# The fourth mixer in another order: index scores first, then the latent, then eight heads' queries between the rounds of the choice

## The chip, the core and the metric

The kernel runs on one core of a Trainium2 chip. TensorE (PE in the profile, its weight loads PEld) multiplies matrices into PSUM banks; VectorE (DVE), ScalarE (ACT) and GpSimd (POOL) do the element-wise work; SyncE (SP) issues the transfers from HBM. Each engine has its own queue of instructions and works it off strictly in order; an instruction waits until what it reads is written and the buffer that it writes is free. The metric is the device time of one execution in microseconds (us). The kernel before took 1725.35 us (median of 3 runs, 1724.01 to 1725.73).

## The reference

Two networks are computed one after the other, two layers each, on 256 tokens of width 1024 (272 tokens in the second network, which puts 16 learned tokens in front). Each layer has a mixer and a gated feed-forward block. The change is in the mixer of the last layer, the fourth mixer of the program. What it computes, cut to what matters:

```python
c_q, c_kv, k_idx, w_idx = split(h @ w_in, [256, 512, 576])
c_q, c_kv = rms_norm(c_q, g0), rms_norm(c_kv, g1)
q_abs, q_idx = split(c_q @ w_uq, [16 * 256])          # 16 heads of 256; 8 index heads of 64
q_abs = rms_norm(q_abs.reshape(b, t, 16, 256), q_norm)
k_idx = rms_norm(k_idx)
act = relu(einsum("bqhd,bsd->bqhs", q_idx, k_idx) * 64 ** -0.5)
score = where(visible, einsum("bqh,bqhs->bqs", w_idx * 8 ** -0.5, act), -1e30)
_, sel = top_k(score, 64)                              # 64 keys for each query
kv = gather(c_kv, sel)
logits = einsum("bqhr,bqkr->bqhk", q_abs, kv) / 16 + bias
p = softmax(where(visible, logits, -1e30))
o = einsum("bqhr,hrd->bqhd", einsum("bqhk,bqkr->bqhr", p, kv), w_uv)
h = h + o @ w_out
```

So a query of the attention (`q_abs`) needs only `c_q`. The scores need `c_q`, `k_idx` and `w_idx`. The latent `c_kv` is needed for the logits and the values, and the choice of 64 keys only for the softmax.

## The kernel before

All activations lie feature by token. Weights come in chunks of up to 1 MB in the order of `stream_plan`; three chunk buffers (`raw`) hold them, five pairs of buffers hold the pieces of up to 1024 columns after they are split into a high part `wh` (ACT, L189) and a low part `wl` (L191, on DVE, or on POOL for the pieces that `ON_POOL` lists). A product of two float32 matrices is three matmuls (`mm3`, L214 to L216). `take` hands out the next piece, `ahead` splits up to four pieces beyond it.

`dsa_mix` is the fourth mixer. It has eight PSUM banks: `mm` 2, `s` 2, `b` 1, `n` 1, `o` 2. In its text it does in turn:

- `c_q`: matmuls with `bw`, scaling (`latent`), sum of squares, norm, split into `cqh` and `cql`.
- The index key `ki` with `bwi`, and its norm over 64 features (matmul with `blk` into an `n` bank).
- The latent `c_kv` with `bw2` (two matrices of 24 matmuls each): scaled into `lat` by DVE, squares, norm, a product on POOL, then `ckg` (keys with all gains) and `ckv` (split, for the values).
- The index weights `wi` with `bwx`, transposed into `wc`.
- The index queries `qi` with `uqi`, and the scores: for each of 8 index heads two matmuls (L222) into an `s` and an `o` bank, relu on ACT (`rl`, L1086), and a weighted sum on DVE (`sc`, L1091 and L1093).
- The choice: eight rounds (`top_rounds`), each with MAX8 and MATCH_REPLACE8 on both halves of the queries (L1106, L1107). Where a score was taken out, `msk` is 1e30 afterwards (L1216, L1217).
- `prep(h)`, one head's query: 12 matmuls into an `mm` bank, squares on ACT with their sums in `qst` (L1150), the inverse root by `rsq`, scaling out of the bank into `qx` (ACT for a head with `h < 2`, L1154, else DVE, L1156), four transposes on PE (L1160, bank `n`), and a copy into `q` on ACT (L1162). The bank stays taken from the first matmul to the scaling, so two heads can be under way.
- `rsq` has two ways. With `pool` set, ACT computes a logarithm, a second small term (L253) and an exponential, POOL does three tiny products (L257 to L259) and DVE the last step (L260). Without it DVE does three steps (L263 to L265).
- `values(g)`: the values of four heads, three products of 6 matmuls and copies on ACT (L1123, L1126).
- `mask(h)`: the bias tile `nb` of a head comes by DMA (three buffers), and POOL adds `msk` (L1167).
- `attend(h)`: logits into an `s` bank (L1179), bias and row minimum on DVE (L1181), exponential on ACT (L1183), reciprocal on DVE (L1185), product on POOL (L1187), transposes into bank `b` (L979 to L982), copy `pr` on ACT (L984), and for each second head the product with the values (`o`, L222).

Before the change the text has the first four heads' queries one by one between pairs of rounds, then `values(0)`, and the loop over the heads prepares head h + 4 (`LAG`) beside head h. The order in the text isn't the order on the engines: the program is built with a scheduler that puts the instructions in an order for each engine by its own estimate of times, and that order is then fixed.

## Time and profile before

| | |
|---|---|
| time, median of 3 | 1725.35 us |
| the profiled execution | 1724.67 us |
| its span, first to last instruction | 1722.9 us |
| mean granted clock of TensorE | 0.991 |
| fourth mixer, first to last matmul | 1379.7 us to 1523.3 us of the span |
| in it: longest time without a matmul | 5.63 us, from 1411.45 us |

The profiled execution lies 0.68 us under the median; 1.77 us of it lie outside the span. TensorE is busy nearly everywhere. The mixer is some 140 us of the span, and what a change in it is worth is read there: at which places TensorE has no matmul to do, and what it waited for. A clock of 0.5 in a row means that TensorE was granted the lower of its two levels (1.2 GHz), 1.0 the higher (2.4 GHz).

### The profile page before, as it was taken

How to read it: one execution, taken by the hardware profiler on the slowest of the kernel's cores; microseconds unless marked ns; L12 is line 12 of the kernel's file. 1: busy time of each engine (PE TensorE's matmuls, PEld its weight loads, DVE VectorE, ACT ScalarE, POOL GpSimd, SP SyncE). 2: the span in 40 equal slices, each digit the busy share in tenths (PEclk: the TensorE clock that was granted, in tenths of full speed). 3: DMA queues.
4: the chain of work that ended last, by engine and by line, in shares of the span. 5: the costliest groups of instructions: out<-in, count | busy, mean ns of one | idle time of the engine just before them, and what ended most of it. 6: DMA issues, size and time to landing. Idle time of an engine off the chain costs nothing.

```text
span 1722.9 us, 32907 instructions
## 1 busy us (share of the span) xinstructions
PE 1682.0 (98%) x13474; PEld 1638.4 (95%) x13474; DVE 1095.4 (64%) x1789; ACT 898.6 (52%) x1559; POOL 417.9 (24%) x426
## 2 busy tenths in 40 slices
PE   8999999999999999999999999999999989999999
PEld 7999999988999999999997899999999978889999
DVE  7757666565666566655787666556665586566653
ACT  6545455476544554444576554444444457755442
POOL 3023220013322022211333522211221135342210
PEclk9999999999999999999999999999999999999999
DMA  7456655434455545444542354454555433345552
GB/s 278 145 189 229 228 194 177 169 105 141 160 183 194 176 171 192 174 171 172 187 145 67 135 184 172 172 176 172 178 177 180 143 112 108 111 151 192 185 189 92
DMA packets 59926, 287.54 MB, mean 167 GB/s; under 512 B 12112, under 2 KB 22864, under 8 KB 29184
## 3 DMA queue, kind: packets, MB, share of 16 engines
q1 hardware_dynamic: 58944, 284.80, 47.7%
q8 instruction: 105, 1.72, 0.4%
q10 hardware_dynamic: 832, 0.66, 0.1%
q14 instruction: 45, 0.37, 0.1%
HBM read 284.34 MB, written 5.53 MB: 168 GB/s over the span
## 4 chain that ended last, share of the span: by engine, by line
PE 93%; DVE 3%; ACT 1%; issue 1%; DMA 1%; SPq 0%; POOL 0%; ACTq 0%; DVEq 0%; POOLq 0%
PE mm L214 21%; PE mm L215 21%; PE mm L216 21%; PE z L216 7%; PE z L215 7%; PE z L214 7%; DVE xl L231 1%; PE s L1179 1%; PE o L222 1%; PE z L222 1%; DMA X<-in_xT_dram 1%; PE s L222 1%; PE o L918 0%; PE n L849 0%; DVE X L390 0%
## 5 line engine op out<-in xcount | busy, mean ns | idle before, releaser
L189 ACT CAST wh<-raw 128x1024 fp32r<-128x1024 f32 (+1 forms) x526 | 541.9, 1032 | 622.9 <-PE mm L215 409.7
L191 DVE TENSOR_TENSOR wl<-raw,wh 128x1024 fp32r<-128x1024 f32 (+2 forms) x494 | 600.3, 1217 | 322.0 <-ACT wh L189 318.2
L214 PE MATMUL mm<-xh,wh 128*128 128x256 f32 (+1 forms) x1808 | 523.9, 290 | 15.1 <-ACT xh L226 4.7
L215 PE MATMUL mm<-xl,wh 128*128 128x256 f32 (+1 forms) x1808 | 520.2, 288 | 0.7 <-DVE xl L231 0.4
L216 PE MATMUL mm<-xh,wl 128*128 128x256 f32 (+1 forms) x1808 | 519.9, 288 | 0.0
L214 PEld LDWEIGHTS mm<-xh,wh 128*128 128x128 f32 x1808 | 342.8, 190 | 21.8 <-ACT xh L226 5.3
L215 PEld LDWEIGHTS mm<-xl,wh 128*128 128x128 f32 x1808 | 342.6, 190 | 5.1 <-issue 2.3
L216 PEld LDWEIGHTS mm<-xh,wl 128*128 128x128 f32 x1808 | 343.5, 190 | 1.0 <-issue 0.5
L215 PE MATMUL z<-xl,wh 128*128 128x256 f32 (+1 forms) x1056 | 302.0, 286 | 1.4 <-DVE xl L231 1.3
L216 PE MATMUL z<-xh,wl 128*128 128x256 f32 (+1 forms) x1056 | 302.0, 286 | 0.0
L214 PE MATMUL z<-xh,wh 128*128 128x256 f32 (+1 forms) x1056 | 301.2, 285 | 0.0
L214 PE MATMUL mm<-gh,wh 128*128 128x256 f32 (+1 forms) x1056 | 300.5, 285 | 0.0
L216 PE MATMUL mm<-gh,wl 128*128 128x256 f32 (+1 forms) x1056 | 299.5, 284 | 0.0
L215 PE MATMUL mm<-gl,wh 128*128 128x256 f32 (+1 forms) x1056 | 299.5, 284 | 0.0
L346 POOL TENSOR_TENSOR es<-es,r 128x256 f32<-128x256 f32 (+1 forms) x110 | 152.4, 1387 | 476.2 <-ACT es L345 476.2
L215 PEld LDWEIGHTS z<-xl,wh 128*128 128x128 f32 x1056 | 199.1, 189 | 2.0 <-DVE xl L231 1.9
L216 PEld LDWEIGHTS z<-xh,wl 128*128 128x128 f32 x1056 | 199.7, 189 | 0.2
L214 PEld LDWEIGHTS z<-xh,wh 128*128 128x128 f32 x1056 | 199.6, 189 | 0.1
L215 PEld LDWEIGHTS mm<-gl,wh 128*128 128x128 f32 x1056 | 199.2, 189 | 0.0
L216 PEld LDWEIGHTS mm<-gh,wl 128*128 128x128 f32 x1056 | 198.5, 188 | 0.0
L214 PEld LDWEIGHTS mm<-gh,wh 128*128 128x128 f32 x1056 | 198.3, 188 | 0.0
L347 DVE TENSOR_TENSOR ea<-z,es 128x256 f32<-128x256 f32 (+1 forms) x132 | 57.1, 433 | 97.7 <-POOL es L346 49.0
(361 smaller groups left out, 1846.1 us busy)
## 6 DMA issues: line engine op xcount, KB each, us to landing
raw<-in_gu_dram SPq DMA_DIRECT2D x132, 1024.0 KB, 4.8
raw<-in_wd_dram SPq DMA_DIRECT2D x66, 1024.0 KB, 4.8
raw<-in_aw_dram SPq DMA_DIRECT2D x12, 1024.0 KB, 4.8
raw<-in_a_in_dram SPq DMA_DIRECT2D x9, 1024.0 KB, 5.3
raw<-in_wo_dram SPq DMA_DIRECT2D x12, 768.0 KB, 4.2
nb<-scr SPq DMA_DIRECT2D x32, 136.0 KB, 2.2
scr<-relrow SPq DMA_DIRECT2D x16, 271.5 KB, 5.3
raw<-in_mkv_dram SPq DMA_DIRECT2D x4, 1024.0 KB, 5.0
```

What stands on the lines that cost most here:

```text
L189: self.nc.scalar.copy(h[:, :c], t[:, x : x + c])
L191: eng.tensor_tensor(l[:, :c], t[:, x : x + c], h[:, :c].bitcast(F32), ALU.subtract)
L214: mm(out, wh, xh, start=first, stop=False, skip_group_check=chk)
L215: mm(out, wh, xl, start=False, stop=False, skip_group_check=chk)
L216: mm(out, wl, xh, start=False, stop=last, skip_group_check=chk)
L222: self.nc.tensor.matmul(out, w, x, start=start, stop=stop, skip_group_check=True)
L231: self.nc.vector.scalar_tensor_tensor(l, src, col, h.bitcast(F32), ALU.mult, ALU.subtract)
L346: nc.gpsimd.tensor_tensor(s, s, r, ALU.mult)
L347: nc.vector.tensor_tensor(a, B[:, :cols], s, ALU.mult)
L1179: nc.tensor.matmul(s[:, c], q[:, k, qc], ckg[:, k, k0 : k0 + n], start=k == 0, stop=k == 1)
```

## The change

- The latent with `bw2` moves in the text from behind the index key to behind the scores, ahead of the queries. Its weights move in the stream from the third place to behind `uqi`.
- All of the first eight heads' queries stand between the rounds of the choice: two ahead of them, two behind each pair of rounds (`LAG` 8 in place of 4). `values(0)` comes behind the last round.
- These eight heads take the `pool` way of `rsq` and are scaled by ACT (before: two heads). In that way the last step moves from DVE to POOL, with one more small instruction on ACT.
- POOL splits the weights of the first eight heads' queries (four pieces, before two) and the first piece of the value weights.

```diff
-ON_POOL = {("uq", 0, 0), ("uq", 1, 0), ("bw2", 0, 0), ("bw2", 0, 1)}
+ON_POOL = {("uq", j, 0) for j in range(4)} | {("bw2", 0, 0), ("bw2", 0, 1), ("uv", 0, 0)}
...
-    put("bw2", 1, 2048)
     put("bwx", 1, 64)
     put("uqi", 1, 1024)
-    put("uq", 2, 1024)
+    put("bw2", 1, 2048)
+    put("uq", 4, 1024)
     put("uv", 1, 512)
...
         if pool:
             tt = nc.gpsimd.tensor_tensor
+            nc.scalar.activation(out, t, AF.Copy, scale=1.5)
             tt(u, u, t, ALU.mult)
             tt(u, u, t, ALU.mult)
             tt(u, u, t, ALU.mult)
-            nc.vector.scalar_tensor_tensor(out, t, 1.5, u, ALU.mult, ALU.add)
+            tt(out, out, u, ALU.add)
...
-        NH, LAG, NB = 16, 4, 3
+        NH, LAG, NB = 16, 8, 3
...
-            bk = self.dense("bw2", xp, T)
-            self.ahead()
-            xs, r = latent(bk, 0, T, p1)
...
+            stage.close()
+            pt = self.pool("dsa", 2, ctx=ctx, reuse_waits="tile")
+            bk = self.dense("bw2", xp, T)
+            self.ahead()
+            xs, r = latent(bk, 0, T, p1)
...
-                self.rsq(st, st, 256, tmp=(pt, "q", 2), pool=h < 2)
+                self.rsq(st, st, 256, tmp=(pt, "q", 2), pool=h < LAG)
                 for tt in range(2):
-                    if h < 2:
+                    if h < LAG:
                         nc.scalar.activation(qx[:, tt], b3[:, tt], AF.Copy, scale=st[:, tt : tt + 1])
...
             prep(0)
-            top_rounds(0, 2)
             prep(1)
-            top_rounds(2, 4)
-            prep(2)
-            top_rounds(4, 6)
-            prep(3)
+            for i in range(4):
+                top_rounds(2 * i, 2 * i + 2)
+                if i < 3:
+                    prep(2 + 2 * i)
+                    prep(3 + 2 * i)
             values(0)
-            top_rounds(6, 8)
```

What the scheduler makes of it, at three places. First TensorE, behind the products of the index key. In the kernel before, the sum of squares of the index key (`n_16203`) stands between the two halves of the latent (`mm_16213` and `mm_16238`):

```order
L214 MATMUL mm_16213<-xh_16016,wh_16001 128x272
L215 MATMUL mm_16213<-xl_16017,wh_16001 128x272
L216 MATMUL mm_16213<-xh_16016,wl_16002 128x272
L1042 MATMUL n_16203<-kq_16201,blk 128x272
L214 MATMUL mm_16238<-xh_16016,wh_16131 128x272
L215 MATMUL mm_16238<-xl_16017,wh_16131 128x272
L216 MATMUL mm_16238<-xh_16016,wl_16132 128x272
```

In the changed kernel, at the same place (`mm_16213` is now the index weights, `mm_16247` and `mm_16255` are index queries, which read `cqh` and `cql`):

```order
L213 MATMUL mm_16213<-xh_16016,wh_16001 8x256
L214 MATMUL mm_16213<-xl_16017,wh_16001 8x256
L215 MATMUL mm_16213<-xh_16016,wl_16002 8x256
L1042 MATMUL n_16203<-kq_16201,blk 128x272
L213 MATMUL mm_16247<-cqh_16076,wh_16133 128x256
L213 MATMUL mm_16255<-cqh_16076,wh_16133 128x256
L1065 MATMUL n_16285<-ident,wi 128x8 x2
L214 MATMUL mm_16247<-cql_16077,wh_16133 128x256
```

The 48 matmuls of the latent have moved from here to behind the third group of scores; what follows the index weights at once are products that need the normed `c_q`.

Second POOL, around the end of the choice. In the kernel before (`qnr` belongs to the queries of heads 0 and 1, `nb` to the masks of heads 0 and 1):

```order
L257 TENSOR_TENSOR qnr_2381_16529<-qnr_2381_16529,qnr_16528 128x2
L258 TENSOR_TENSOR qnr_2381_16529<-qnr_2381_16529,qnr_16528 128x2
L259 TENSOR_TENSOR qnr_2381_16529<-qnr_2381_16529,qnr_16528 128x2
L1167 TENSOR_TENSOR nb_16689<-nb_16689,msk_16442 128x144
L1167 TENSOR_TENSOR nb_16689<-nb_16689,msk_16442 128x272
L1167 TENSOR_TENSOR nb_16695<-nb_16695,msk_16442 128x144
```

In the changed kernel (`qnr_2388` and `qst_16562` belong to head 2's query, `lat` to the latent):

```order
L1105 TENSOR_TENSOR lat_2349_16420<-lat_2349_16420,latr_2354_16429 128x272
L257 TENSOR_TENSOR qnr_2388_16566<-qnr_2388_16566,qnr_16565 128x2
L258 TENSOR_TENSOR qnr_2388_16566<-qnr_2388_16566,qnr_16565 128x2
L1169 TENSOR_TENSOR nb_16853<-nb_16853,msk_16350 128x144
L1169 TENSOR_TENSOR nb_16853<-nb_16853,msk_16350 128x272
L1169 TENSOR_TENSOR nb_16859<-nb_16859,msk_16350 128x144
L259 TENSOR_TENSOR qnr_2388_16566<-qnr_2388_16566,qnr_16565 128x2
L1169 TENSOR_TENSOR nb_16859<-nb_16859,msk_16350 128x272
L1169 TENSOR_TENSOR nb_16898<-nb_16898,msk_16350 128x144
L1169 TENSOR_TENSOR nb_16898<-nb_16898,msk_16350 128x272
L1110 COPY ckvh_16078<-ckvh_16078 128x2x32
L260 TENSOR_TENSOR qst_16562<-qst_16562,qnr_2388_16566 128x2
```

Head 2's query, which had no work on POOL before, now has its third and fourth step there behind the masks, and the masks read `msk`, the result of the choice.

Third ACT, at the first heads' attention in the changed kernel (`qx_16561` is head 2's query, `q_16582` its copy, `qx_16651` head 4's):

```order
L1185 ACTIVATE L_2361_16454,ast_16904<-L_2361_16454,ast_16904 128x144
L1185 ACTIVATE L_2361_16454,ast_16904<-L_2361_16454,ast_16904 128x272
L1156 ACTIVATE qx_16561<-mm_16548,qst_16562 128x256 x2
L252 ACTIVATE qnr_2398_16608<-qst_16604,neps 128x2
L1185 ACTIVATE L_2362_16455,ast_17000<-L_2362_16455,ast_17000 128x144
L1185 ACTIVATE L_2362_16455,ast_17000<-L_2362_16455,ast_17000 128x272
L256 ACTIVATE qst_16604<-qnr_16607 128x2
L1164 COPY q_16582<-n_16577 128x512
L1152 ACTIVATE qx_16651,qst_16652<-mm_16638 128x256 x2
```

The scaling of head 2 (L1156), the small term (L252) and the new copy (L256) stand in ACT's queue between the exponentials (L1185) of heads 0 and 1; before, none of these three was there for head 2.

## Rows read from the trace of the kernel before

**Rows 1.** The page: busy time, share of the span and instructions of each engine.
```profile
PE 1682.0 (98%) x13474; PEld 1638.4 (95%) x13474; DVE 1095.4 (64%) x1789; ACT 898.6 (52%) x1559; POOL 417.9 (24%) x426
```

**Rows 2.** Stretches: us, busy of each engine (instructions), granted clock, DMA share, GB/s.
```profile
972.00:975.40 3.40, 3.40 (x20) 3.40 (x20) 1.98 (x5) 1.73 (x4) 2.88 (x3) 0.65 0.08 29
...
1411.40:1417.10 5.70, 0.07 (x2) 0.03 (x1) 5.70 (x22) 4.07 (x16) 0.59 (x3) 0.79 0.45 110
1417.10:1425.00 7.90, 7.90 (x45) 7.51 (x46) 7.90 (x42) 4.53 (x17) 0.59 (x3) 0.72 0.09 36
```

**Rows 3.** Timeline of PE: start, us, line, what, count, idle before and its releaser.
```profile
970.09 0.39 PE L214 MATMUL mm<-xh,wh 128*128 128x272 f32 x1 [3.75 <-ACT xh L226]
...
1400.34 0.28 PE L214 MATMUL mm<-cqh,wh 128*128 128x256 f32 x1
...
1417.08 1.27 PE L1160 MATMUL n<-ident,qx 128*128 128x128 f32 x4 [5.63 <-ACT qx L1154]
...
1420.70 1.98 PE L1179 MATMUL s<-ckg,q 128*128 128x144 f32 x8
...
1422.88 0.37 PE L214 MATMUL mm<-wh,cqh 128*128 128x256 f32 x1
...
1424.37 1.57 PE L1179 MATMUL s<-ckg,q 128*128 128x144 f32 x8
...
1429.52 1.67 PE L1179 MATMUL s<-ckg,q 128*128 128x144 f32 x8 [0.70 <-DVE ast L1181]
...
1456.71 1.67 PE L1179 MATMUL s<-ckg,q 128*128 128x144 f32 x8
...
1468.09 1.31 PE L222 MATMUL o<-pr,v 128*64 128x256 f32 x16 [1.37 <-ACT pr L984]
```

**Rows 4.** Timeline of DVE, from the norm of `c_q` to the first head's logits.
```profile
1392.04 0.42 DVE L263 SCALAR_TENSOR_TENSOR nr<-o,nr 128x256 f32<-128x256 f32 x1 [1.66 <-ACT nr L254]
1392.50 1.13 DVE L264 SCALAR_TENSOR_TENSOR nr<-nr,nr 128x256 f32<-128x256 f32 x1
...
1395.82 2.28 DVE L227 TENSOR_TENSOR cql<-ea,cqh 128x256 fp32r<-128x256 f32 x2 [0.60 <-ACT cqh L226]
...
1413.43 0.44 DVE L1106 MAX8 m<-sc 128x8 f32<-128x272 f32 x1
1413.78 1.21 DVE L191 TENSOR_TENSOR wl<-raw,wh 128x1024 fp32r<-128x1024 f32 x1
...
1424.84 0.44 DVE L1216 TENSOR_TENSOR msk<-wk,sc 128x272 f32<-128x272 f32 x1
...
1428.29 0.31 DVE L1181 CUSTOM_DVE_ANT_0 L<-s,nb 128x144 f32<-128x144 f32 x1 [0.38 <-POOL nb L1167]
```

**Rows 5.** Timeline of POOL, the same stretch.
```profile
1390.94 2.41 POOL L191 TENSOR_TENSOR wl<-raw,wh 128x1024 fp32r<-128x1024 f32 x1 [7.54 <-PE o L288]
1394.87 2.61 POOL L191 TENSOR_TENSOR wl<-raw,wh 128x1024 fp32r<-128x1024 f32 x1 [1.52 <-DVE ea L1025]
...
1415.45 0.20 POOL L257 TENSOR_TENSOR qnr<-qnr,qnr 128x2 f32<-128x2 f32 x1 [4.45 <-ACT qnr L254]
1415.72 0.20 POOL L258 TENSOR_TENSOR qnr<-qnr,qnr 128x2 f32<-128x2 f32 x1
...
1426.85 4.46 POOL L1167 TENSOR_TENSOR nb<-nb,msk 128x144 f32<-128x144 f32 x6 [8.19 <-DVE msk L1217]
```

**Rows 6.** Timeline of ACT, the first score and head 0's scaling.
```profile
1404.46 0.52 ACT L1086 ACTIVATE rl<-s 128x416 f32<-128x416 f32 x1 [0.54 <-PE s L222]
...
1416.55 0.84 ACT L1154 ACTIVATE qx<-mm,qst 128x256 f32<-128x256 f32 x2 [1.18 <-DVE qst L260]
```

**Rows 7.** Groups of ACT by line, 1426 to 1503 us: count, busy us, mean ns.
```profile
L1183 ACT ACTIVATE L<-L,ast 128x144 f32<-128x144 f32 (+1 forms) x31 | 14.4, 466 | 8.0 <-DVE ast L1181 7.7
...
L1150 ACT ACTIVATE qx<-mm 128x256 f32<-128x256 f32 x24 | 9.0, 382 | 2.9 <-PE mm L216 2.9
...
L1162 ACT COPY q<-n 128x512 f32<-128x512 f32 x14 | 8.1, 581 | 2.5 <-PE n L1160 2.4
```

More of the change, by code (lines that the diff above doesn't have):

```diff
@@ L115, in stream_plan @@
     put("bwi", 1, 1024)
-    put("bw2", 1, 2048)
     put("bwx", 1, 64)
     put("uqi", 1, 1024)
-    put("uq", 2, 1024)
+    put("bw2", 1, 2048)
+    put("uq", 4, 1024)
     put("uv", 1, 512)
-    put("uq", 1, 1024, 2)
+    put("uq", 1, 1024, 4)
     put("uv", 1, 512, 1)
-    put("uq", 2, 1024, 3)
+    put("uq", 2, 1024, 5)
     put("uv", 1, 512, 2)
-    put("uq", 2, 1024, 5)
+    put("uq", 1, 1024, 7)
     put("uv", 1, 512, 3)
-    put("uq", 1, 1024, 7)
     wo(3)
@@ L1044, in dsa_mix @@
             nc.vector.scalar_tensor_tensor(ki, ki, 0.125, kq, ALU.mult, ALU.mult)
-            bk = self.dense("bw2", xp, T)
-            self.ahead()
-            xs, r = latent(bk, 0, T, p1)
-            for k in range(2):
-                nc.gpsimd.tensor_tensor(xs[k], xs[k], r, ALU.mult)
-                nc.vector.tensor_scalar(ckg[:, k, P:], xs[k], gk[:, k : k + 1], None, ALU.mult)
-                self.split_scaled(ckv[0][:, k, 32:], ckv[1][:, k, 32:], xs[k], self.g("ckv", k))
-            nc.scalar.copy(ckg[:, :, :P], ckg[:, :, P + NM : P + NM + P])
-            for i in range(2):
-                nc.gpsimd.tensor_copy(ckv[i][:, :, :32], ckv[i][:, :, 32:64])
             w = self.take("bwx", KD)
@@ L1107, in top_rounds @@
                         nc.vector.match_replace(wk[:, c], m8, src[:, c], -HUGE)
+            stage.close()
[3 more added lines that the diff above has]
+            xs, r = latent(bk, 0, T, p1)
+            for k in range(2):
+                nc.gpsimd.tensor_tensor(xs[k], xs[k], r, ALU.mult)
+                nc.vector.tensor_scalar(ckg[:, k, P:], xs[k], gk[:, k : k + 1], None, ALU.mult)
+                self.split_scaled(ckv[0][:, k, 32:], ckv[1][:, k, 32:], xs[k], self.g("ckv", k))
+            nc.scalar.copy(ckg[:, :, :P], ckg[:, :, P + NM : P + NM + P])
+            for i in range(2):
+                nc.gpsimd.tensor_copy(ckv[i][:, :, :32], ckv[i][:, :, 32:64])
             vs = [self.t(p1, [P, 4, S], f"v{i}") for i in range(2)]
@@ L1199, in attend @@
                     self.pair_out(y, h // 2, o)
-            stage.close()
-            pt = self.pool("dsa", 2, ctx=ctx, reuse_waits="tile")
             Ls = [self.t(pt, [P, W], f"L{e}", bufs=1) for e in range(2)]
```

## Prediction

> **What bounds the kernel now.** First the page's busy times: TensorE is busy 98% of the span [rows 1], so a change in order can only give back the rest, or add to it. Then the stretches of this mixer and the timeline of TensorE. The matmuls of the mixer are the same before and after; its time is their work plus the holes between them. The one big hole is at the choice: nothing for 5.63 us until the first head's transposes start at 1417.08, which waited for the scaled query of head 0 [rows 3]. Behind it the granted clock is 0.79 and 0.72 in the stretches [rows 2]: head 2's 12 matmuls and head 0's logits are slow. A head's 12 matmuls take 1.49 us at the full clock (1422.88 to 1424.37) and head 0's logits 1.98 against 1.57 us [rows 3]; with the query of head 2 and its transposes I put the loss by the clock at 2.0 us. Smaller holes, 0.70 and 1.37 us, follow at 1428.8 and 1466.7 [rows 3]. Without holes and at full clock the mixer could be 10 to 12 us shorter; no order of it can bring more.
>
> Why the hole is there is read from DVE's timeline: the rounds run from 1413.43 to 1424.84 without a pause, with one weight split of 1.21 us in them [rows 4], so one round takes (11.41 - 1.21) / 8 = 1.28 us. The first logits are used by DVE only at 1428.29, after the mask on POOL, which could start at 1426.85 [rows 4, 5]. So the chain scores, choice, mask, first softmax sets the attention's start, and matmuls that don't depend on it are what can fill TensorE meanwhile. That is what the change rearranges.
>
> **The change, part by part.** I follow the chain by times of the trace of before and the new orders of the engines.
>
> *Start of the scores.* Before, TensorE goes from the index key through the latent and the index weights without a pause to the index queries at 1400.34 [rows 3], and the normed `c_q` is ready by then: its last split ends at 1395.82 + 2.28 = 1398.10 [rows 4]. After, the latent's 48 matmuls (48 x 0.125 = 6.0 us by the pace of a head's 12) and one small sum (0.4) are gone from there, so TensorE has done all at about 1400.3 - 6.4 = 1393.9. The next product needs `cqh`. That wait is new, and it isn't short, since DVE stands still while POOL splits weights: the step at 1392.50 took 1.13 us where its sister at 1392.04 took 0.42, and ended as POOL's split ended (1390.94 + 2.41 = 1393.35); the split of `cql` took 2.28 us for two beside POOL's 2.61 us [rows 4, 5]. After the change the latent's weights come two pieces later in the stream, and their buffers are the ones that the `c_q` products give back; I estimate POOL's two splits of them from 1386.8 on, just ahead of those of the first two query pieces: four splits of 2.4 us, to about 1397.0. The products by DVE that lead to `c_q` fall between and behind them; I put `cqh` at 1397.8 and `cql` at 1399.5. A new hole of 3.9 us (at least 1.3, if `c_q` is ready as early as now, at 1395.2 to 1396 for its high part). Index queries and the first score product then take until 1401.9, and the first relu starts at 1402.4 in place of 1404.46 [rows 6]: 2.1 us earlier. Bounds: 0.5 us later than before, if the clock falls behind the new hole, to 4 us earlier.
>
> The clock is one end of that: a hole of 3.75 us elsewhere in this trace (until 970.09) is followed by a granted clock of 0.65 in the stretch 972.0 to 975.4 [rows 2, 3]. At the low level the index queries and scores, 5.6 us of matmuls, would take some 2.6 us more.
>
> *Scores and choice.* From the first relu's end (1404.98 [rows 6]) to the first round (1413.43 [rows 4]) it is 8.4 us now. The latent's steps and a weight split on DVE leave this stretch (2.6, estimated from the 0.4 of such a step and half of the split of 1.21), but POOL's split of the third query piece comes into it, 2.4 us in which I count DVE as held. So 8.2 us from 1402.9: first round at 1411.1, 2.3 us earlier than now. Into the rounds come, on DVE, two scalings of the latent (0.35 each, one ahead of the first round), a split of 1.2 and the latent's norm of three steps of 0.4: 10.2 + 0.35 + 1.2 + 1.2 = 12.95 us, end at 1424.0, 0.8 us earlier than now. The small steps of the queries, 6 x 0.07, leave them.
>
> The Trainium skill ("SBUF — State Buffer", section "Who interferes with whom") says that a VectorE instruction with two SBUF inputs and a GpSimd instruction that reads SBUF exclude each other for the whole of an instruction, and that VectorE with one SBUF input is untouched. The trace agrees as far as it shows it: 1.13 us with two inputs in SBUF against 0.42 us with one in PSUM, both beside the same POOL split [rows 4, 5]. By this rule MAX8 and MATCH_REPLACE8 are not held by POOL's 2.4 us and 1.2 us splits that now fall into the rounds; no row of before shows such a pair.
>
> *What fills the rounds.* TensorE has the latent (48 matmuls, 6 us), done by 1410.7, mostly between the score products. Then queries, and here the text of the change and the order differ: a query holds one of two `mm` banks until it is scaled, and head 0's bank is free only when DVE has taken the latent out, behind the last score at 1411. Before, head 0's 12 matmuls stood between the score products. From 1411 head 0's chain is squares 0.73, logarithm and exponential 0.6, POOL four steps of 0.28 [rows 5], ACT's scaling 0.84 [rows 6]; but on ACT a split, the latent's squares and head 1's squares stand between, so head 0's transposes come at about 1418.9, head 1's at 1421.9. Head 2's third step on POOL is queued behind the masks, that is behind the choice. So two heads' queries are done by the end of the choice, with matmuls for four: as many as before, not eight. Holes in TensorE: 0.8, 3.3, 0.7 and 2.9 us, up to 1427.3.
>
> *The first softmax.* Behind the choice stand on DVE the mask (0.75 + 0.4) and the latent's `ckg`, which POOL's product (2 x 0.75) precedes; ACT's copy ends at 1427.1; logits of head 0 from 1427.3, DVE takes them at 1428.2. Before: 1428.29. So the chain gains nothing, and TensorE has less behind it: head 1's logits (1.4), head 2's transposes (0.5) and 12 value matmuls (1.4) are done by then before, and not after: 3.3 us of debt.
>
> *Heads 2 to 7.* ACT has for each head two exponentials 0.93 (14.4 / 15.5), squares 0.75 (9.0 / 12), two copies of 0.58 [rows 7], logarithm and exponential 0.4, half a weight split 0.5: 3.7 us. The change adds the scaling 0.73, the small term 0.2 and the new copy 0.2: 4.8 us by durations, 4.65 by starts, since neighbours overlap a little. TensorE's query, transposes, logits and transposes of the weights are 1.49 + 0.45 + 1.4 + 0.45 = 3.8 us a head. So ACT paces these heads, and beyond that each query waits in POOL's queue behind masks and products (6 mask halves took 4.46 us [rows 5]). I walked heads 2 to 7 through the three queues: 5.3 us a head, with logits of head 7 at 1460.3, against 1456.71 now [rows 3]. Bounds: 3.8 (TensorE) to 6.5. At that moment TensorE has done less than before at its own: by the orders 24 value matmuls (2.9), half of two pairs' outputs (as much as one of 1.31 [rows 3]) and one set of transposes (0.4) are missing: 4.6 us. DVE gets 1.3 us a head back, which nobody waits for, being busy less than ACT there.
>
> *Sum.* 1460.3 - 1456.7 = 3.6, plus debt 4.6, less half of the hole of 1.37 us that the debt may fill [rows 3]: +7.5 us. From there to the end both have the same work, and heads 8 to 15 take the same way as before. SP's queue: the query weights go out earlier and the bias tiles behind them, still some 15 us ahead of the masks: nothing. The end of the mixer (norm for the last feed-forward) changes order slightly; I take 0, with 2 us either way. 1724.67 + 7.5 = 1732.2 for an execution like the profiled one; the median lies 0.7 higher: 1732.9.
>
> **The rivals.**
>
> *No change.* ACT's queue is not hurt by POOL's (4.65 us a head, 6 x 0.65 = 3.9 less) and POOL's split doesn't hold DVE in the scores (2.4 less): +1.2, 1726.6. For it: before, ACT's waits for POOL's results are short. Against: POOL's order puts the query's steps behind masks that come late.
>
> *Faster: the hole closes and TensorE paces everything.* Choice over at 1419.7 (`c_q` as early as now 1.9, POOL holds nothing 2.4), logits of head 0 at 1423.0, then 7 x 3.8 us: head 7 at 1449.6, which is -7.1, debt +4.6, the 1.37 filled: -3.9, 1721.5. For it: 5.63 us and a lost clock are there to be gained. Against: the new hole is certain by TensorE's order, only its size is open.
>
> *Slower by more.* the choice itself is held up: TensorE's clock falls behind the new hole of 3.9 us as it did behind the one of 3.75 (2.6 us on the score path), and POOL's two splits hold DVE in the rounds too (2.4 + 1.2): +13.7, 1739.1. For it: both effects are seen elsewhere in the trace; against: MAX8 has one input. It decides from the point where the choice ends later than now, at 1424.84.
>
> *The change doesn't do what it says.* It is part of the forecast already: the order shows two heads' queries done in the rounds.
>
> **How the numbers follow.** Forecast 0.50, no change 0.19, faster 0.12, slower by more 0.19. The measurement can tell 0.2% from nothing, 3.5 us. The forecast and its own spread (1729 to 1737) and the worse case give slower 0.68; no change and a bit of the forecast's low end 0.20; faster 0.12. The range reaches from 1722 (the faster case left out for the most part) to 1740.
>
> **What would show it.** A new hole in TensorE at about 1394, ended by ACT's `cqh` or DVE's `cql`; POOL at work without a pause from 1387 to 1397; the first MAX8 at 1411 and the first `msk` at 1424; head 0's transposes not before 1417; ACT over 90% busy from 1430 to 1460 with TensorE waiting for `qx` and `q`; head 7's logits at 1460. I am wrong if the choice ends before 1421, or if heads 2 to 7 come at less than 4.5 us a head; then the time is at or under the present one.

## The result, and the profile after

The changed kernel takes 1737.92 us (median of 4 runs, 1735.49 to 1738.98) against 1724.68 us (1722.34 to 1725.73) of the kernel before on the same chip: a ratio of 1.0066, 95% interval 1.0049 to 1.0084. It is slower, as forecast, by 13.2 us where 7.5 were forecast, and within the range given. The profiled execution took 1738.13 us, with a span of 1736.4, so the difference of the two profiled executions (13.46 us) may be read for that of the medians (13.24 us).

TensorE's busy line on the page answers to [rows 1]: the same 13474 matmuls take 8.1 us more busy time.
```profile
PE 1690.1 (97%) x13474; PEld 1642.7 (95%) x13474; DVE 1086.8 (63%) x1754; ACT 905.5 (52%) x1585; POOL 426.1 (25%) x455
```
TensorE's timeline of the changed kernel, at the places of [rows 3]:
```profile
1386.19 0.39 PE L213 MATMUL mm<-xh,wh 128*128 128x272 f32 x1 [0.17 <-DVE lat L1013]
...
1397.74 0.79 PE L213 MATMUL mm<-cqh,wh 128*128 128x256 f32 x2 [4.14 <-ACT cqh L225]
...
1402.89 0.82 PE L221 MATMUL s<-ki,qi 64*128 64x272 f32 x1
...
1421.02 1.24 PE L1162 MATMUL n<-ident,qx 128*128 128x128 f32 x4 [2.43 <-ACT qx L1156]
...
1429.41 0.39 PE L1181 MATMUL s<-ckg,q 128*128 128x144 f32 x1 [2.66 <-ACT ckg L1108]
...
1440.00 0.33 PE L1162 MATMUL n<-ident,qx 128*128 128x128 f32 x1 [1.96 <-ACT qx L1156]
...
1451.69 1.19 PE L1162 MATMUL n<-ident,qx 128*128 128x128 f32 x4 [2.04 <-ACT qx L1156]
...
1466.47 0.76 PE L1181 MATMUL s<-ckg,q 128*128 128x144 f32 x4
...
1542.51 0.55 PE L213 MATMUL mm<-xh,wh 128*128 128x256 f32 x1 [2.49 <-DVE X L390]
```
The one hole of 5.63 us at the choice is gone. In its place stand 4.14 us ahead of the index queries, 2.43 at the choice, 2.66 ahead of head 0's logits, and one of 0.4 to 2.0 us ahead of the next heads' transposes, which wait for the scaled query `qx`. Head 0's logits start at 1429.41 (1420.70 before), head 7's at 1466.47 (1456.71), and the first matmuls behind the mixer's last hole at 1542.51 (1528.45 before).

The stretches of the changed kernel (us, busy time and instructions of PE, PEld, DVE, ACT, POOL, granted clock, DMA share, GB/s), to be held against [rows 2]; the last two lines are the stretch of heads 2 to 7:
```profile
1392.00:1397.50 5.50, 1.60 (x12) 0.94 (x10) 5.27 (x6) 2.31 (x5) 4.61 (x2) 1.00 0.55 191
1397.50:1404.50 7.00, 6.73 (x28) 5.54 (x28) 2.39 (x8) 1.70 (x5) 0.00 (x0) 0.51 0.14 40
...
1435.00:1445.00 10.00, 7.17 (x51) 6.01 (x49) 1.64 (x11) 7.90 (x26) 6.15 (x15) 1.00 0.16 37
1445.00:1457.00 12.00, 9.69 (x54) 8.39 (x55) 2.17 (x9) 8.16 (x32) 5.71 (x16) 0.86 0.30 81
```
Behind the new hole the granted clock is 0.51, which is the lower of the two levels (1.2 of 2.4 GHz), for all of the index queries and the first score product. From 1435 to 1457 no engine is busy throughout: TensorE 72% and 81%, ACT 79% and 68%, POOL 62% and 48%, DVE 16% and 18%. The same two stretches of the kernel before had TensorE at 98% and 93%:
```profile
1435.00:1445.00 10.00, 9.80 (x84) 9.00 (x83) 4.52 (x16) 8.96 (x29) 6.29 (x12) 1.00 0.30 78
1445.00:1457.00 12.00, 11.13 (x87) 9.54 (x87) 9.74 (x37) 9.93 (x39) 3.75 (x6) 1.00 0.65 207
```
The timelines of the changed kernel on DVE, then POOL, then ACT, for [rows 4 to 6]:
```profile
1392.16 0.42 DVE L263 SCALAR_TENSOR_TENSOR nr<-o,nr 128x256 f32<-128x256 f32 x1 [2.19 <-ACT nr L253]
1392.62 1.49 DVE L264 SCALAR_TENSOR_TENSOR nr<-nr,nr 128x256 f32<-128x256 f32 x1
...
1407.22 5.88 DVE L1083 SCALAR_TENSOR_TENSOR sc<-rl,wc,sc 128x272 f32<-128x272 f32 x12 [0.78 <-ACT rl L1076]
...
1413.56 0.66 DVE L1096 MAX8 m<-sc 128x8 f32<-128x272 f32 x2
...
1425.00 0.42 DVE L265 SCALAR_TENSOR_TENSOR latr<-nr,nr 128x272 f32<-128x272 f32 x1
...
1426.04 1.40 DVE L1215 TENSOR_TENSOR msk<-wk,sc 128x272 f32<-128x272 f32 x3
1427.36 0.35 DVE L1106 TENSOR_SCALAR ckg<-lat,gk 128x272 f32<-128x272 f32 x1
```
```profile
1386.71 7.11 POOL L190 TENSOR_TENSOR wl<-raw,wh 128x1024 fp32r<-128x1024 f32 x3 [6.14 <-ACT wh L188]
1394.18 2.79 POOL L190 TENSOR_TENSOR wl<-raw,wh 128x1024 fp32r<-128x1024 f32 x1 [0.36 <-DVE nr L264]
1406.57 2.37 POOL L190 TENSOR_TENSOR wl<-raw,wh 128x1024 fp32r<-128x1024 f32 x1 [9.60 <-ACT wh L188]
...
1413.30 3.66 POOL L190 TENSOR_TENSOR wl<-raw,wh 128x1024 fp32r<-128x1024 f32 x2 [2.33 <-ACT wh L188]
```
```profile
1404.63 0.52 ACT L1076 ACTIVATE rl<-s 128x416 f32<-128x416 f32 x1 [1.27 <-PE s L221]
```
POOL splits four pieces from 1386.71 to 1396.97, and the norm of `c_q` on DVE stands beside them: its second step takes 1.49 us where the first takes 0.42. The first relu, forecast 2.1 us earlier, comes at 1404.63 (1404.46 before); the first MAX8 at 1413.56 (1413.43); the first mask instruction at 1426.04 (1424.84).

### The profile page after: what moved, and what is told of

Same layout as the page of the kernel before. It is cut to its first block, busy times and chain, and to the rows that moved or that the text cites. A ratio compares the mean times of both kernels' runs of the same rounds, so it can differ in the third digit from the quotient of the medians.

```text
span 1736.4 us, 32941 instructions
## 1 busy us (share of the span) xinstructions
PE 1690.1 (97%) x13474; PEld 1642.7 (95%) x13474; DVE 1086.8 (63%) x1754; ACT 905.5 (52%) x1585; POOL 426.1 (25%) x455
## 4 chain that ended last, share of the span: by engine, by line
PE 93%; DVE 4%; ACT 2%; issue 1%; DMA 1%; POOL 1%; ACTq 0%; POOLq 0%; DVEq 0%
PE mm L213 21%; PE mm L214 21%; PE mm L215 21%; PE z L215 7%; PE z L214 7%; PE z L213 7%; PE o L221 1%; DVE xl L230 1%; PE s L1181 1%; PE s L221 1%; PE z L221 1%; DMA X<-in_xT_dram 1%; PE o L918 0%; PE n L849 0%; DVE X L390 0%
## 5 line engine op out<-in xcount | busy, mean ns | idle before, releaser
L190 DVE TENSOR_TENSOR wl<-raw,wh 128x1024 fp32r<-128x1024 f32 (+3 forms) x491 | 597.8, 1219 | 319.4 <-ACT wh L188 316.7
L346 POOL TENSOR_TENSOR es<-es,r 128x256 f32<-128x256 f32 (+1 forms) x110 | 152.3, 1387 | 476.0 <-ACT es L345 476.0
```

The costliest lines, as they stand in the source:

```text
L190: eng.tensor_tensor(l[:, :c], t[:, x : x + c], h[:, :c].bitcast(F32), ALU.subtract)
L346: nc.gpsimd.tensor_tensor(s, s, r, ALU.mult)
```

## The experiments

Each ratio is to the kernel before on the same chip, with its 95% interval: for the changed kernel from 4 runs beside 4, for the others from 5 to 12 beside 14 to 34. For the profiles one table serves all: us from the first matmul behind the hole at 1383 to 1387 (1386.19 in the changed kernel's rows, 1386.61 before) to the first relu, the first MAX8, head 0's logits (s0), from there to head 7's (s7), on to the matmul behind the mixer's last long hole, and their sum, the mixer. The stages ahead are the same in all kernels and end up to 4 us apart, so starts are counted from that matmul. The last column says how far the profiled execution lies from the median of its kernel.
```
                           relu  MAX8    s0  s0-s7  s7-end  mixer   ratio    off
before                     17.8  26.8  34.1   36.0    71.7  141.8  1       -0.7
after                      18.4  27.4  43.2   37.1    76.0  156.3  1.0066  +0.2
e1 latent back             19.1  29.1  35.9   40.4    76.3  152.6  1.0049  -2.8
e2 root, scaling back      17.0  25.9  41.8   30.3    75.4  147.6  1.0024  -2.7
e3 both back               19.1  29.1  36.0   31.3    76.0  143.3  0.9987  -0.5
e4 after, hole filled      15.9  24.8  40.6   38.7    76.1  155.4  1.0047  +3.9
e5 root back               17.0  25.9  41.8   30.4    76.3  148.5  1.0025  -1.7
e6 scaling back            17.0  25.9  41.8   34.8    76.2  152.8  1.0046  -3.2
e7 e2, hole filled         15.9  24.8  40.7   30.3    75.5  146.5  1.0006  -0.6
e8 e3, choice filled       19.1  29.1  34.6   31.9    76.0  142.5  0.9985  -0.3
e9 e3, list of before      17.9  26.9  34.1   31.3    76.0  141.5  0.9977  +0.8
e10 before, roots on POOL  17.8  26.8  34.1   46.4    69.1  149.6  1.0014  +1.8
e11 after, old root        18.3  27.2  43.1   36.9    73.4  153.4  1.0036  +0.1
e12 e9, choice filled      17.9  26.9  32.7   31.7    76.0  140.4  0.9964  -2.2
```
The mixer is the same work in all of them, about 1005 matmuls besides idle ones. Its parts are not: from s0 to s7 TensorE does 254 matmuls in the kernel before and e10, 216 in e2, e7 and e11, 210 in e1, e3, e8, e9 and e12, and 194 in the others. A profile is one execution, and some lie 2 to 4 us from their kernel's median; where a price is read from profiles, the ratios are given beside it.

**e1: the latent ahead of the index scores again** (with its weights' place in the stream), all else as changed:
```
             nc.vector.scalar_tensor_tensor(ki, ki, 0.125, kq, ALU.mult, ALU.mult)
+            bk = self.dense("bw2", xp, T)
+            ...
-            bk = self.dense("bw2", xp, T)
-            ...
```


> The changed kernel, but the latent and its weights stand where they stood before the change (behind the index key). Everything else is as changed: eight heads' queries between the rounds, their root on POOL, their scaling on ACT. Theory A (both parts cost: the hole of 4.1 us ahead of the index queries with the clock lost behind it, and the queries of heads 2 to 7 held up in the queues of POOL and ACT): 5 us over the kernel before, 1729.7, no hole at 1394, heads 2 to 7 at 5 us or more each. Theory B (only the hole and the clock cost): as before, 1724.7. Theory C (only the queries of heads 2 to 7 cost): as changed, 1738.

**e2: roots and scaling of heads 2 to 7 on DVE again**, all else as changed:
```
-                self.rsq(st, st, 256, tmp=(pt, "q", 2), pool=h < LAG)
+                self.rsq(st, st, 256, tmp=(pt, "q", 2), pool=h < 2)
-                    if h < LAG:
+                    if h < 2:
```


> The changed kernel, but only heads 0 and 1 take the way over POOL and are scaled by ACT, as before the change; heads 2 to 7 go over DVE. Theory A: 7 us over the kernel before, 1731.7; the hole at 1394 and the low clock stay, heads 2 to 7 come at about 4.5 us each. Theory B: as changed, 1738. Theory C: as before, 1724.7.

**e3: both edits.**

> Both undone: the latent at its old place, and only heads 0 and 1 over POOL. What is left of the change: the order of the queries and the rounds in the text, LAG 8, and POOL's splits of the weights. All three theories: as before, 1724.7 within 2.5 us. If it is 5 us or more over it, the order of the queries costs by itself and all three are incomplete.

Measured: e1 1734.51 us, 1.0049 (1.0030 to 1.0068); e2 1730.46, 1.0024 (1.0012 to 1.0037); e3 1724.45, 0.9987 (0.9976 to 0.9997); before 1725.94. Both edits together undo the loss, and e1 and e2 each leave a part of it that is clear of the kernel before, so theory A holds in kind. B falls by both; C falls by e2, since e1's interval still takes in the changed kernel's 1.0066. The shares of A were the wrong way round: the part that heads 2 to 7 pay is the larger, 9.2 us of mixer from e3 to e1 and 8.7 from e2 to the changed kernel (10.7 and 7.2 us by the ratios); the latent's move costs 4.3 us from e3 to e2 and 3.8 from e1 to the changed kernel (6.4 and 2.9). Of the 8.7 us, 1.4 lie ahead of the first relu, where TensorE, DVE, ACT and POOL do the same instructions in the same order in both kernels; they are a difference of the granted clock between two executions, not of the roots.

**e4: idle matmuls in the new hole**, 7 of 128x256 float32 that nothing reads, on the root of `c_q`'s norm (its tile is called `latr`, like the latent's; the trace shows two rows for each):
```
+            fill = self.bank("b")
+            for k in range(7):
+                nc.tensor.matmul(fill[:, :S], rr[:, :P], rr, start=True, stop=True)
             qi = self.t(pa, [P, 4, S], "qi")
```


> The changed kernel with 7 idle float32 products (128x256, the norm of c_q, into a bank that is free there) in TensorE's queue in the hole ahead of the index queries; nothing reads them. Theory A with the clock as part of the cost: the granted clock stays at 1.0 from 1397.6 on, the first relu comes at about 1402.5 in place of 1404.6, and the time falls by 2 to 4 us to 1735. If the hole costs only its own length: 1738, since the hole's end is set by c_q and not by TensorE.

Measured: 1734.13 us, 1.0047 (1.0031 to 1.0062). TensorE's timeline of e4 and its stretches:
```profile
1395.33 3.29 PE L1057 MATMUL b<-latr 128*128 128x256 f32 x14 [1.21 <-DVE latr L265]
1398.27 0.58 PE L213 MATMUL mm<-cqh,wh 128*128 128x256 f32 x2
...
1401.58 0.49 PE L221 MATMUL s<-ki,qi 64*128 64x272 f32 x1
```
```profile
1394.00:1401.00 7.00, 5.56 (x31) 4.73 (x31) 6.39 (x12) 2.99 (x7) 3.12 (x2) 1.00 0.46 156
1401.00:1404.00 3.00, 3.00 (x26) 2.45 (x26) 0.85 (x3) 1.77 (x4) 0.00 (x0) 1.00 0.00 0
...
1427.35:1466.02 38.67, 33.03 (x195) 27.87 (x195) 9.90 (x40) 26.75 (x96) 22.44 (x57) 0.87 0.26 66
```
The index queries start as late as in the changed kernel (11.55 us from the common start in both), but at full clock: a score product takes 0.49 us in place of 0.82, and the first relu is 2.6 us earlier, as the forecast's price of the clock had it (2.6). So is head 0 (40.6 against 43.2). At head 7 only 1.0 us of it is left in this execution (79.3 against 80.3). But this execution lies 3.9 us above the median of e4, and from head 0 to head 7 its granted clock is 0.87, where the changed kernel's profiled execution does as many instructions on every engine at 0.95:
```profile
1429.41:1466.47 37.06, 30.01 (x195) 24.96 (x195) 9.95 (x40) 27.07 (x96) 22.48 (x57) 0.95 0.27 69
```
So how much of the 2.6 us the filled hole keeps up to head 7 isn't shown. By the ratios e4 gains some 3 us on the changed kernel, as the forecast for it had it (2 to 4), with intervals that overlap.

**e5 and e6: the two halves of e2**, root or scaling of heads 2 to 7 back on DVE:
```
-                self.rsq(st, st, 256, tmp=(pt, "q", 2), pool=h < LAG)
+                self.rsq(st, st, 256, tmp=(pt, "q", 2), pool=h < 2)
```
```
-                    if h < LAG:
+                    if h < 2:
```


> The changed kernel with one edit: the roots of heads 2 to 7 are refined by VectorE again (three instructions of it), while the scaling of all eight heads stays on ScalarE. The first four kernels showed that root and scaling together cost 7 us here (1.0066 to 1.0024 of the kernel before). Theory R (the root costs: its four GpSimd instructions stand in GpSimd's queue behind the masks and the probabilities' scaling, ScalarE waits for them, and it has a copy more to do): most of the 7 us is given back, ratio 1.003 to 1.004, 1731 us beside 1725, and through heads 2 to 7 GpSimd's qst is no longer what ends ScalarE's idle time. Theory S (the scaling costs: two more ScalarE instructions of 0.42 us a head): at most 1.5 us is given back, ratio 1.006, 1735.5 us. Both halves needed at once: some 3.5 us, 1.0045.

> The changed kernel with the other edit alone: VectorE scales the queries of heads 2 to 7 again, while all eight roots stay on GpSimd. Theory R (the root costs): at most 1.5 us is given back, ratio 1.006, 1735.5 us beside 1725; VectorE, busy with the rounds of the choice and the masks' sums, may even give it later. Theory S (the scaling costs): most of the 7 us is given back, 1.003, 1731 us.

Measured: e5 1730.49 us, 1.0025 (1.0015 to 1.0036); e6 1735.02, 1.0046 (1.0031 to 1.0062). e5 gives back what e2 did, with ACT still scaling all eight heads: theory R. e6 lies below R's figure (1.006), on that of "both halves at once", which e5 rules out; its interval takes in R's figure and begins just above the 1.003 of theory S. So the root carries the loss, and whether the scaling on ACT adds a part of its own isn't settled.

**e10: the kernel before with the roots of heads 2 to 7 on POOL:**
```
-                self.rsq(st, st, 256, tmp=(pt, "q", 2), pool=h < 2)
+                self.rsq(st, st, 256, tmp=(pt, "q", 2), pool=h < 8)
```


> The kernel before with one edit: the roots of heads 2 to 7 are refined by GpSimd (three instructions, VectorE does the last one, as for heads 0 and 1 there). Everything else is as before. Theory Q (a root that GpSimd refines stands behind the masks and the probabilities in its queue, wherever the heads' queries are issued): heads 4 to 7 are paced as in the changed kernel, 3 to 7 us more, ratio 1.002 to 1.004, 1730 us beside 1725.5, and from a head's squares to its transposes it takes over 7 us for heads 4 to 6 (5.2, 3.9 and 6.0 before). Rival E (it costs only where eight heads' queries are issued ahead): within 1 us, 0.9995 to 1.0005.

Measured: 1730.51 us, 1.0014 (1.0000 to 1.0027), which takes in Q's lower end (1.002) and rival E's upper end (1.0005); the twelve executions fall in two groups, four at 1723.5 to 1725.5 us and eight at 1729.1 to 1732.9, and the profiled one (1732.33) is of the second. Its mixer is 7.7 us longer than before. POOL's timeline at head 3's root (`qnr`), then DVE's, and what TensorE waits for:
```profile
1427.19 4.46 POOL L1167 TENSOR_TENSOR nb<-nb,msk 128x144 f32<-128x144 f32 x6 [3.45 <-DVE msk L1217]
1431.62 0.19 POOL L257 TENSOR_TENSOR qnr<-qnr,qnr 128x2 f32<-128x2 f32 x1
...
1435.06 0.69 POOL L259 TENSOR_TENSOR qnr<-qnr,qnr 128x2 f32<-128x2 f32 x1
1435.71 1.19 POOL L1167 TENSOR_TENSOR nb<-nb,msk 128x144 f32<-128x144 f32 x2
1436.87 1.01 POOL L1187 TENSOR_TENSOR L<-L,ast 128x144 f32<-128x144 f32 x2
1437.85 1.19 POOL L1167 TENSOR_TENSOR nb<-nb,msk 128x144 f32<-128x144 f32 x2
```
```profile
1435.78 3.28 DVE L260 SCALAR_TENSOR_TENSOR qst<-qnr,qnr 128x2 f32<-128x2 f32 x1
```
```profile
1439.63 0.48 PE L1160 MATMUL n<-ident,qx 128*128 128x128 f32 x1 [4.39 <-DVE qx L1156]
```
Two things hold head 3 here. Its three instructions of 0.2 to 0.7 us take POOL from 1431.62 to 1435.75, behind 4.46 us of masks. Then the last step, on DVE, takes 3.28 us where most others of its kind take 0.14 to 0.16: it ends as POOL ends a run of six masks and products (1435.71 to 1439.04), and TensorE's 4.39 us without a matmul end only behind it. The second thing can't happen to heads 0 to 7 of the changed kernel, where POOL does the last step. The delay falls on heads 3 and 4 (13.8 and 11.7 us from squares to transposes), not on 4 to 6 as Q had it (11.7, 4.3, 6.5). So e10 shows that a root on POOL can hold up a head outside the change, but in part by another way than the queue, and its price there isn't settled.

In the changed kernel all four steps of a root are on POOL. Head 3's, the rest of the rows between them being masks and products:
```profile
1434.18 0.20 POOL L257 TENSOR_TENSOR qnr<-qnr,qnr 128x2 f32<-128x2 f32 x1
1434.33 0.50 POOL L1169 TENSOR_TENSOR nb<-nb,msk 128x144 f32<-128x144 f32 x1
1434.79 0.20 POOL L258 TENSOR_TENSOR qnr<-qnr,qnr 128x2 f32<-128x2 f32 x1
...
1436.10 0.20 POOL L259 TENSOR_TENSOR qnr<-qnr,qnr 128x2 f32<-128x2 f32 x1
...
1436.85 1.21 POOL L1169 TENSOR_TENSOR nb<-nb,msk 128x144 f32<-128x144 f32 x2
1438.00 0.20 POOL L260 TENSOR_TENSOR qst<-qst,qnr 128x2 f32<-128x2 f32 x1
```
Four instructions of 0.20 us take 4.0 us of POOL's queue; those of heads 2 and 4 to 7 take between 1.7 (head 4) and 5.8 us (head 2). In e5 DVE does its three for head 4 within 1.47 us:
```profile
1435.47 0.43 DVE L263 SCALAR_TENSOR_TENSOR qnr<-qst,qnr 128x2 f32<-128x2 f32 x1 [1.14 <-ACT qnr L253]
...
1436.53 0.41 DVE L265 SCALAR_TENSOR_TENSOR qst<-qnr,qnr 128x2 f32<-128x2 f32 x1
```
From the end of ACT's squares to the first transpose, heads 4, 5 and 6 need 8.4, 8.3 and 9.5 us in the changed kernel and 4.5, 8.6 and 10.6 in e6, but 4.4, 3.0 and 4.2 in e2 and 4.1, 4.9 and 5.9 in e5 (5.2, 3.9 and 6.0 before). Heads 2, 3 and 7 don't show it so: 7.9, 12.1 and 6.9 us in the changed kernel, 9.3, 10.2 and 7.7 in e2.

**e11: the changed kernel with the root's old form** (DVE does the last step):
```
-            nc.scalar.activation(out, t, AF.Copy, scale=1.5)
-            tt(out, out, u, ALU.add)
+            nc.vector.scalar_tensor_tensor(out, t, 1.5, u, ALU.mult, ALU.add)
```


> The changed kernel with the root's formula as before: VectorE does the last step of it, in place of ScalarE's copy and GpSimd's fourth instruction. Theory Q (GpSimd's queue sets the time, three instructions there or four): 1 to 2 us less at most, ratio 1.005 to 1.006, 1735 us beside 1725.5. Rival F (the new formula, with one more instruction on ScalarE and a further handover, is what costs): most of the 7 us is given back, 1.0025 to 1.0035, 1730.5 us.

Measured: 1734.57 us, 1.0036 (1.0024 to 1.0048). The interval takes in F's figures and leaves out Q's: by the ratios the longer form costs 5 of the 7 us. The profiles give it 2.9 us of mixer where e2 has 8.7 (7.3 without the clock ahead of the first relu). s0 to s7 takes as long as in the changed kernel (36.9 against 37.1), with 216 matmuls in it in place of 194. So the longer form is a part of the loss; how large a part, and whether by POOL's fourth instruction or by ACT's copy, isn't settled.

**e7: e2 with e4's idle matmuls.**

> The changed kernel with roots and scaling of heads 2 to 7 on VectorE (as in e2, ratio 1.0024), and seven matmuls of 128x256 float32 on the latent's root that nothing reads, which fill the hole ahead of the index queries. Moving the latent alone costs 6 us here (e3 to e2). Theory H (that cost is the hole ahead of the index queries and the half clock behind it): with the hole filled and nothing downstream to hide it, the head start of 2.6 us that the filled kernel e4 had at head 0's scores is kept to the end: ratio 1.0005 to 1.0012, 1727 us beside 1725. Rival K (head 0's scores wait for the latent's product with the gain, which now comes after the choice has begun, and this is the whole of it): no gain, 1.0024, 1729.5.

Measured: 1727.19 us, 1.0006 (0.9994 to 1.0019), theory H's figure. The profile is more modest: 1.1 us at the first relu, kept to the end of the mixer, since the clock cost e2's profiled execution less than the changed kernel's (17.0 against 18.4 us to the first relu). A hole of 3.12 us ahead of head 0's logits stays. The reason for it stands in the changed kernel's DVE rows above: the latent's root (1425.00) is queued between the rounds, its product with the gain `ckg` (1427.36) behind the mask. Of the 4.3 us that the latent's move costs, 1.1 are the clock by the profiles; the rest goes with this second wait, the one that K names, by these rows, but no run took it away alone. The ratios would give the clock more (3 us, with intervals that overlap), so the split between the two isn't settled.

**e8: e3 with idle matmuls at the choice; e9: e3 with the list of POOL's pieces as before; e12: e9 with idle matmuls at the choice.**
```
+                if h == 1:
+                    fill = self.bank("b")
+                    for _ in range(42):
+                        nc.tensor.matmul(fill[:, :S], ckv[0][:, 1, 32 : 32 + P], ckv[0][:, 1, 32 : 32 + S], start=True, stop=True)
```
```
-ON_POOL = {("uq", j, 0) for j in range(4)} | {("bw2", 0, 0), ("bw2", 0, 1), ("uv", 0, 0)}
+ON_POOL = {("uq", 0, 0), ("uq", 1, 0), ("bw2", 0, 0), ("bw2", 0, 1)}
```


> Candidate: latent ahead of the index scores as before, roots and scaling of heads 2 to 7 on VectorE (e3, ratio 0.9987), and 42 matmuls of 128x256 that nothing reads, issued after head 1's query matmuls, in the hole of 6.3 us at the choice. In e3 the granted clock was at its lower level for 10.2 us from 1413.6 us on, and TensorE worked for 5.7 us of them. If those matmuls hold the clock at its upper level, head 0's to head 2's work takes half the time there: 2 to 3 us, ratio 0.997 to 0.9975, 1721.5 us beside 1725. Rival: the choice's rounds on VectorE set the pace there anyway, so that nothing is gained: 0.9987, 1723. Rival on the other side: the idle matmuls run past the moment at which head 0's query is ready, and the half clock comes later all the same: 1.000 to 1.001.

> The kernel e3 (latent ahead of the index scores, roots and scaling of heads 2 to 7 on VectorE; ratio 0.9987) with the list of weight pieces that GpSimd splits as in the kernel before: pieces 2 and 3 of the queries' weights and the first of the values' weights go back to VectorE. Theory N (this list is no part of the cost: GpSimd has room in this order, VectorE too): 0.998 to 0.9995, 1723.5 us beside 1725.5. Rival V (VectorE paces the choice, and three splits of 1.2 us each on it come on top): 1.000 to 1.002, 1727. Rival W (GpSimd's splits slow VectorE's sums, and without them the scores come earlier): 0.997, 1720.5.

> The fastest version so far (e9: eight heads' queries between the rounds as in the change, all else as in the kernel before; ratio 0.9977), with 36 matmuls of 128x256 that nothing reads in the hole of 5.6 us at the choice. In e9 the granted clock was at its lower level for 6.8 us from 1414.8 us on. Theory C (what the clock gives back there is needed by nothing, since the next heads' scores still wait for the query's chain through ScalarE and GpSimd): no gain, as from e3 to e8, 0.997 to 0.9985, 1723 us beside 1726. Rival H (the work behind the hole goes at full clock and is kept, as from e2 to e7): 2 to 3 us, 0.996, 1720.5 us. Rival on the other side (36 idle matmuls and the values' and later products find the bank taken): 0.999.

Measured: e8 1723.46 us, 0.9985 (0.9975 to 0.9995); e9 1723.86, 0.9977 (0.9964 to 0.9991); e12 (36 idle matmuls) 1721.30, 0.9964 (0.9952 to 0.9976), with 1727.76 before. e8's ratio is that of e3, the figure of the rival that nothing is gained; its profile gains 0.8 us of mixer. e9 isn't told from e3 by its ratio; in the profile its first MAX8 is 2.2 us earlier and the mixer 1.9 us shorter, in W's direction. In e3 a POOL split of 2.39 us at 1397.42 stands beside the second step of the index key's norm, which takes DVE 2.54 us (0.44 in e9); the scaling of the latent out of its bank comes behind it, and TensorE waits for that bank for 1.02 us, a hole that e9 doesn't have. V is wrong. The choice in e9, then in e12:
```profile
1411.50:1417.10 5.60, 0.07 (x1) 0.00 (x0) 5.60 (x21) 4.49 (x18) 0.78 (x4) 0.79 0.24 69
1417.10:1423.00 5.90, 5.85 (x29) 5.46 (x29) 5.90 (x29) 3.51 (x13) 0.78 (x4) 0.62 0.36 107
```
```profile
1408.30:1413.90 5.60, 4.32 (x37) 4.11 (x35) 5.59 (x21) 4.49 (x18) 0.78 (x4) 1.00 0.28 77
1413.90:1419.80 5.90, 5.85 (x44) 5.46 (x45) 5.90 (x32) 4.33 (x15) 0.78 (x4) 1.00 0.36 108
```
With the idle matmuls the granted clock stays at 1.00, and TensorE does 44 matmuls in 5.9 us where it did 29. Of the 1.5 us that head 0 gains by it, 1.0 reach the end of the mixer. The ratio lies between C's figures and H's; its interval takes in H's 0.996 and C's lower end, 0.997, and overlaps e9's. e12 beats both kernels: 6.5 us less than before. The profiles put 1.4 us of that into this mixer; 3.2 us lie ahead of the common start, where no edit reaches, in a profiled execution that is the fastest of e12's nine. Where the rest lies isn't settled.

## Why the prediction was right, and where its sizes were off

The sign and the two causes were right: the new hole, and roots that POOL refines, though how much of their price is POOL's queue and how much the longer form (e11) is open. Taken back one after the other, the parts of the 14.5 us of mixer are 8.7 for the roots and the scaling (changed kernel less e2; 1.4 of it is the clock), 4.3 for the latent (e2 less e3), 1.9 for the pieces on POOL (e3 less e9), and -0.4 for the rest of the change, the eight heads' queries between the rounds above all (e9 less before; its ratio, 0.9977, says -4). By e1 the first two are 9.2 and 3.8, so they hardly depend on the order.

- *The new hole*: 3.9 us to 1397.8 forecast, 4.14 us to 1397.74 measured, with POOL's four splits and DVE held beside them as worked out. Right.
- *The start of the scores*: forecast 2.1 us earlier, measured 0.2 later. This step failed. The clock fell behind the hole; the working had the price, 2.6 us, from the hole of 3.75 us at 970 [rows 2, 3] (at that row's 0.65 throughout, 5.6 us of matmuls would take 3.0 us more), but put it into the worse case instead of the sum, although its own row was the nearest to the case. e4 shows it: with the hole filled the first relu comes 2.6 us earlier. How much is lost differs between executions: e2 does the same instructions up to the first relu and reaches it 1.4 us earlier than the changed kernel.
- *Scores and choice*: from first relu to first MAX8 8.93 us (8.7 forecast), the rounds and what lies in them 12.48 (12.95). POOL's split held DVE's sums: 5.88 us for twelve, which take 0.37 us each in e3 (3.66 for ten). The worse case's other half, that POOL's splits hold the rounds too, was false: beside a POOL split of 3.66 us a pair of MAX8 took 0.66 us, 0.64 later on without one. The Trainium skill ("SBUF — State Buffer", section "Who interferes with whom") says that a VectorE instruction with at most one SBUF input, outside its two-port modes, goes untouched; these rows agree.
- *The first softmax*: forecast 1427.3, measured 1429.41. The 2.1 us are those of the clock, passed on (e4, without them, is 2.6 us earlier at head 0); the wait is `ckg`, as worked out.
- *Heads 2 to 7*: 33.0 us forecast from head 0's to head 7's logits, 37.1 measured, and in steps of 5.9 us (35.55 / 6) from head 1 to head 7 where 5.3 were forecast. The bound of 6.5 held, the reason didn't: ACT was to be over 90% busy, and was 79 and 68%. Of its groups in the changed kernel, 1426 to 1503 us, to be held against [rows 7], the last two lines show who it waited for:
```profile
L1185 ACT ACTIVATE L<-L,ast 128x144 f32<-128x144 f32 (+1 forms) x26 | 12.1, 467 | 1.7 <-DVE ast L1183 1.7
...
L1156 ACT ACTIVATE qx<-mm,qst 128x256 f32<-128x256 f32 x12 | 5.0, 473 | 2.2 <-POOL qst L260 2.2
L248 ACT ACTIVATE qnr<-qst,eps 128x2 f32<-128x2 f32 x13 | 4.0, 305 | 4.2 <-POOL qnr L259 3.2 <-DVE qst L265 1.0
```
This step failed too: the sum of an engine's durations was taken for its pace, and the pace is the round trip of a root through ACT, POOL and ACT again. The wait of L248, the logarithm that begins a root, for POOL's L259 shows why the trips don't overlap: `rsq` has one buffer for each of its two small tiles (`bufs=1`), so a head's root can begin only when POOL has read the last head's. No run gave it a second buffer. e5 shows the cause: with the root on DVE and the scaling still on ACT, s0 to s7 takes 30.4 us for the same 194 matmuls. ACT is 96% busy then, in the stretch 1435 to 1445 us of e5, and TensorE 100%:
```profile
1435.00:1445.00 10.00, 10.00 (x77) 9.44 (x76) 4.98 (x19) 9.57 (x34) 6.23 (x10) 1.00 0.41 109
```
- *The debt*: 4.6 less half a hole of 1.37, so 3.9 us, from head 7 to the end; measured 76.0 less 71.7, 4.3. Near it.

In sum 3.6 became 9.8 us at head 7: 2.1 from the clock and 4.1 from the heads. The time came out at the price of "slower by more" (1739.1), though only half of that case's mechanism took place; that the two figures meet is luck.

## What to carry to other kernels

A chain of tiny instructions should go to an engine whose queue is short at that moment: four instructions of 0.2 us, each behind masks and products of 0.4 to 0.8 us, delayed the queries of heads 4 to 6 by 3 to 5 us, with no engine busy, and no sum of durations shows it. When products are moved away from under a norm that they were hiding, count the hole and the slower clock behind it in the sum, not among the mishaps. What a filled hole or an early choice gives need not reach the end: 1.5 us at head 0 were 0.8 and 1.0 us at the end of the mixer in e8 and e12, while the 1.1 us of e7 were kept. And before a stage's price is read from one profile, look where that execution lies among the runs of its kernel.

## What the runs showed of the hardware

- Idle matmuls in a hole keep the granted clock at its upper level: 1.00 in e4 from 1394 to 1404 us against 0.51 in the changed kernel from 1397.5 to 1404.5, and 1.00 in e12 at the choice against 0.79 and 0.62 in e9. The work behind them started no later in e4.
- The clock's loss behind the same hole differs from execution to execution. e2 has the hole too (4.12 us, to 1396.82), with the same instructions in the same order on TensorE, DVE, ACT and POOL up to the first relu, and this stretch behind it, 0.76 where the changed kernel had 0.51, with its first relu 1.4 us earlier:
```profile
1396.80:1403.80 7.00, 6.94 (x42) 5.84 (x42) 3.12 (x11) 2.98 (x7) 0.00 (x0) 0.76 0.13 40
```
- In e10 a small DVE instruction (128x2, two inputs in SBUF) took 3.28 us beside a run of six masks and products on POOL and ended with the run; most others of its kind take 0.14 to 0.16 us.
- Executions of one kernel differ with the mean granted clock: e4's nine go from 1732.36 us at 0.993 to 1738.57 at 0.989.
